# Two transformer blocks on one core: three stick-breaking half chunks between the delta net's last two transposings, and two small pieces of work moved to later steps

## The chip, the cores and the metric

The kernel runs on one core of one Trainium2 chip. The metric is the device time of one execution in microseconds, shown as the median of three runs. A core has five engines that run side by side and meet only through semaphores: TensorE (PE in the profile, its weight loads PEld), VectorE (DVE), ScalarE (ACT), GpSimd (POOL) and SyncE (SP), which here issues nearly all DMA transfers, in order.

## The reference

The input is 256 tokens of 1024 values, with 16 meta tokens put in front; everything is float32. The first block is a hybrid mixer and a mixture of experts, the second has attention, a pooling mixer and two MLPs. What matters here is the mixer:

```python
proj = x @ w_in
q = l2_normalize(split_heads(q, DN_HEADS)) * (DN_HEAD_DIM ** -0.5)
o_dn = gated_delta_rule_chunked(front(q), front(k), front(v), front(beta), front(g))[:, :, pad:]
o_dn = merge_heads(rms_norm(o_dn, dn_norm_g)) * jax.nn.silu(dn_z.astype(jnp.float32))
o_sb = merge_heads(stick_breaking_attention(q, k, v))
gate = jax.nn.sigmoid(gates.reshape(b, l, N_BRANCH, d) + b_gate)
merged = (gate[:, :, 0] * (o_dn @ w_branch_dn) + gate[:, :, 1] * (o_sb @ w_branch_sb))
return merged @ w_out
```

The delta net (4 heads of 128) and the stick-breaking attention (8 heads of 64) are two branches over the same tokens. Each goes through a projection of its own, `w_branch_dn` and `w_branch_sb`. After a layer norm, 32 experts follow, of which each token takes two.

## The kernel before

Weights stream from memory in chunks of 1 MB (`wraw`), each of two halves. A half is split before use: ACT rounds it to a high part (L324) and DVE takes the remainder (L326); both lie in one of two `wsplit` buffers, and a product is three matmuls (high by high, low by high, high by low: L374, L375, L376). So a half is 24 matmuls, the split of a half waits until the half two places before it has been used, and a chunk's place in the ring is free once its second half is split. SP loads five chunks ahead.

The mixer has three generators, advanced in one loop (L1052 on), a step of each per turn `it`. `F` is the projections that are left (the fill: halves of 24 matmuls that keep PE busy). `M` is the delta net: for two chunks of 128 tokens (and the meta tokens) it builds a triangular matrix, inverts it by seven levels of doubling (`invert`: GpSimd masks the blocks, PE multiplies and transposes, ACT and DVE evacuate), and then walks the two chunks. `sticks` are the four pairs of stick-breaking heads: PE makes the scores, ACT takes exp, exp and log, DVE adds (L923) and scans (L927), GpSimd subtracts (L928), ACT takes exp (L929), PE transposes (L936) and multiplies (L944 to L948).

The root of q's norms, `rq`, is ten small instructions on DVE (`rsqrt`, L437 to L446, and a product, L812). It is written in the step that makes q's norms, although its first reader is the end of a chunk (L894). `router_weights()` folds the first layer norm into the expert router's weights: four matmuls (L994) and five DVE instructions (L995 to L998). It is called in turn 2, and its result is read when the experts begin.

After the loop, each chunk's result `oraw` is multiplied by the gate `zr` (L1069, DVE), transposed (L1072, PE) and split (`odh`, `odl`). `BS_AT` says which of the four half chunks of `w_branch_sb` stand behind the first of these two transposings and which behind the second: `for i in range(BS_AT[c], BS_AT[c + 1])`. With (0, 1, 1) one stands between them and three follow the second. Each of them ends in two evacuations on DVE (`sb_evac`, L957). Eight half chunks of gates follow, then the delta net's branch, the output projection, the layer norm and the experts.

The experts' weights (`wexp`, 99 loads of 1 MB) go into 22 places, which come free one after another while the mixer ends. When all 22 are full, the next load waits for PE to have used the first.

The order on each engine is not that of the code: a scheduler places instructions by their dependencies and its costs, and `tc.issue_after` holds one back until another has been issued. Each engine runs its own list strictly in order.

Of the kernel before, what the change touches and what calls it, by code (L numbers as in the profile page):

```python
# [14 lines left out]
OP = mybir.AluOpType  # L15
# [31 lines left out]
DEPTH = 3  # L47
PARTS = (1, 2, 4, 6, 8)
G_ELSE = (1, 4, 6)
BS_AT = (0, 1, 1)  # L50
COUNT_AT = 0
DN_STEPS = (3, 5, 10, 11, 11)
DN_FILL = (7, 9)
ALPHA = float(np.float32(2.0 ** 0.25))
# [228 lines left out]
def tile_hybrid_block(ctx: ExitStack, tc: tile.TileContext, A, out, dump=None, stop=99):  # L283
    nc = tc.nc
    V, S, G, PE = nc.vector, nc.scalar, nc.gpsimd, nc.tensor
# [36 lines left out]
    def split_into(hi, lo, src, sub=None, after=(None, None)):  # L322
        with tc.issue_after(after[0].ins) if after[0] else nullcontext():
            S.copy(hi, src)  # L324
        with tc.issue_after(after[1].ins) if after[1] else nullcontext():
            (sub or V).tensor_tensor(lo, src, hi.bitcast(F32), op=OP.subtract)  # L326
# [40 lines left out]
    def ws_half(stream, m0, nk, xh, xl, width, fn, newbank):  # L367

        wh, wl = stream.half()
        for q in range(8 // nk):  # L370
            p = newbank()
            for k in range(nk):
                o = (q * nk + k) * 128
                PE.matmul(p[:, :width], wh[:, o:o + 128], xh[:, k, :], start=k == 0, stop=False)  # L374
                PE.matmul(p[:, :width], wl[:, o:o + 128], xh[:, k, :], start=False, stop=False)  # L375
                PE.matmul(p[:, :width], wh[:, o:o + 128], xl[:, k, :], start=False, stop=k == nk - 1)  # L376
            fn(m0 + q, p)
# [53 lines left out]
    def rsqrt(x, shape):  # L431
        P, n = shape
        y = small.tile([128, 12], F32, tag="rs_y", name="rs_y")[:P, :n]
        z = small.tile([128, 12], F32, tag="rs_z", name="rs_z")[:P, :n]
        t = small.tile([128, 12], F32, tag="rs_t", name="rs_t")[:P, :n]
        ti = small.tile([128, 12], I32, tag="rs_i", name="rs_i")[:P, :n]
        V.tensor_scalar(ti, x.bitcast(I32), 1, None, op0=OP.arith_shift_right)  # L437
        V.tensor_scalar(y.bitcast(I32), ti, -1.0, float(0x5F1FFFF9), op0=OP.mult, op1=OP.add)
        V.tensor_tensor(t, y, y, op=OP.mult)
        V.tensor_tensor(t, t, x, op=OP.mult)  # L440
        V.scalar_tensor_tensor(z, t, -RS_A, y, op0=OP.add, op1=OP.mult)
        V.tensor_tensor(t, z, z, op=OP.mult)
        V.tensor_tensor(t, t, x, op=OP.mult)
        V.tensor_scalar(y, t, RS_Q[0], RS_Q[1], op0=OP.mult, op1=OP.add)
        V.tensor_tensor(y, y, t, op=OP.mult)
        V.scalar_tensor_tensor(y, y, RS_Q[2], z, op0=OP.add, op1=OP.mult)  # L446
        return y
# [153 lines left out]
    mark = {}  # L601
# [87 lines left out]
    def delta():  # L689
# [72 lines left out]
        for c in range(2):  # L762
# [7 lines left out]
            for h in range(4):  # L770
                V.scalar_tensor_tensor(di[c][:, HS[h]], pd[:, HS[h]], pc[c][:, 32 + h:33 + h], C("nincl"),
                                       op0=OP.subtract, op1=OP.add)
# [8 lines left out]
        for c in range(2):  # L781
# [7 lines left out]
            for h in range(4):  # L789
                V.scalar_tensor_tensor(At[:, HS[h]], pk[:, HS[h]], pc[c][:, h:h + 1], ds_[:, HS[h]],  # L790
                                       op0=OP.mult, op1=OP.mult)
# [4 lines left out]
        rq = mix.tile([128, 8], F32, name="rq")  # L796
# [11 lines left out]
                PE.matmul(pn[:, c * 4 + h:c * 4 + h + 1], sq[:, META + c * 128:META + c * 128 + 128],  # L808
                          C("ones")[:, 0:1], start=True, stop=True)
        V.tensor_scalar(rq, pn[:, :8], 1e-6, None, op0=OP.add)  # L810
        rq = rsqrt(rq, (128, 8))
        V.tensor_scalar(rq, rq, float(128.0 ** -0.5), None, op0=OP.mult)  # L812

        G.memset(mv_, 0.0)
        G.tensor_copy(mv_.rearrange("p (h c) -> p h c", c=32)[:, :, :16], cvv[:, :, :16])
# [9 lines left out]
        S.copy(mrow, p[:, :256].rearrange("p (a d) -> p a d", d=128))  # L825
        yield
        XTs = [None] * 3
        live = [0, 1, 2]
        while live:
            for i in list(live):  # L830
                r = next(gens[i])
                if r is not None:
                    XTs[i] = r
                    live.remove(i)
            yield
# [16 lines left out]
        for c in range(2):  # L852
# [5 lines left out]
            for h in range(4):  # L858
                V.scalar_tensor_tensor(nR[:, HS[h]], pks[:, HS[h]], pc[c][:, 64 + h:65 + h], vr[c][:, h, :],
                                       op0=OP.mult, op1=OP.subtract)  # L860
# [14 lines left out]
            if c == 0:  # L875
# [4 lines left out]
                for h in range(4):  # L880
                    V.scalar_tensor_tensor(Sn[:, HS[h]], Sst[:, HS[h]], edl[:, c, h:h + 1], pS[:, HS[h]],
                                           op0=OP.mult, op1=OP.add)
# [103 lines left out]
    def router_weights():  # L986

        t = mix.tile([128, 2, 288], F32, tag="zt", name="wr2")
        k36 = lambda a: a.rearrange("p (k n) -> p k n", n=36)
        for q, n in enumerate(("ln1g", "ln1b")):  # L990
            o = _VCOLS[n][0]
            V.tensor_tensor(k36(t[:, q, :]), k36(wrt), colv[:, o:o + 8, None].to_broadcast([128, 8, 36]), op=OP.mult)
            p = bank()
            PE.matmul(p[:, :288], C("ones"), t[:, q, :], start=True, stop=True)  # L994
            V.tensor_reduce(rcb[:, q, :], p[:, :288].rearrange("p (k n) -> p n k", n=36), axis=AX.X, op=OP.add)  # L995
        V.tensor_scalar(rcb[:, 0, :], rcb[:, 0, :], 1.0 / D, None, op0=OP.mult)
        V.tensor_tensor(rcb[:, 1, :], rcb[:, 1, :], rb, op=OP.add)
        V.tensor_tensor(k36(wrt), k36(t[:, 0, :]), rcb[:, None, 0, :].to_broadcast([128, 8, 36]), op=OP.subtract)  # L998
# [14 lines left out]
    def prefetch(n):  # L1013

        while exn[0] < 99 and len(exq) < n and sn[0] - n_slots < (exq[0][0] if exq else sn[0]):
            if ring3[0][0] is None and sn[0] >= 4 + N_RING2:
                break
            i = exn[0]
            exn[0] += 1
            num, t = sn[0], slot()  # L1020
            with tc.issue_after(last_load[0].ins) if last_load[0] else nullcontext():
                if 0 <= i - 12 * SPARE_AT < 3:
                    last_load[0] = spare_load[0](t, i - 12 * SPARE_AT)
                else:
                    g, k = divmod(i if i < 12 * SPARE_AT else i - 3, 12)
                    last_load[0] = nc.sync.dma_start(t, A["wexp"][g, k].rearrange("p e n -> p (e n)"))
            exq.append((num, t))
# [3 lines left out]

    sticks = []
    M = delta()
    F = fill()
    ws_front(wpre, DN_ORDER[:FRONT], hh, hl, T, dn_evac, bank)
    for n, m in enumerate(DN_ORDER):
# [4 lines left out]
        if n in DN_FILL:  # L1041
            next(F)
        for _ in range(DN_STEPS.count(n)):
            next(M)
# [5 lines left out]
    m_on = f_on = True  # L1050
    it = 0
    while m_on or f_on or sticks:  # L1052
        if it == 2:
            router_weights()
        if it >= 8:
            with tc.issue_after(mark["DVE"].ins):
                next(residual_steps, None)
        it += 1
        if m_on:
            m_on = next(M, "end") != "end"  # L1060
        if f_on:
            f_on = next(F, "end") != "end"
        sticks[:] = [s for i, s in enumerate(sticks) if i >= N_STICKS or next(s, "end") != "end"]
        if it > 12 and not sticks and not exq:
            prefetch(4)

    oraw = ofin[0]
    for c in range(2):
# [4 lines left out]
        split_into(odh[:, :, c * 128:(c + 1) * 128], odl[:, :, c * 128:(c + 1) * 128], v3(p))  # L1073
        for i in range(BS_AT[c], BS_AT[c + 1]):
            ws_half(wpre, 2 * i, 4, osh, osl, SEQ, sb_evac, bank)
# [8 lines left out]

    for i in range(BS_AT[2], 4):
        ws_half(wpre, 2 * i, 4, osh, osl, SEQ, sb_evac, bank)
# [74 lines left out]
    def tt(o, a, b, op):  # L1161
# [9 lines left out]
                           op0=OP.is_ge, op1=OP.mult)  # L1171
# [63 lines left out]
    def count_blocks():  # L1235
        cnt = rt([32], "cnt", tag="xact")
        nb = rt([32], "nb", tag="xoff")
        pc_ = bank4()
        PE.matmul(pc_[:, 0:32], C("ones"), msk_[:, 0:32], start=True, stop=False)
        PE.matmul(pc_[:, 0:32], C("ones"), msk_[:, 32:64], start=False, stop=True)  # L1240
        V.tensor_copy(cnt, pc_[:, 0:32])
        V.tensor_scalar(nb, cnt, float(CAP), None, op0=OP.is_gt)
        for m_ in range(2, SEQ // CAP):
            V.scalar_tensor_tensor(nb, cnt, float(CAP * m_), nb, op0=OP.is_gt, op1=OP.add)
        V.tensor_tensor_scan(ci, nb, nb, 0.0, op0=OP.add, op1=OP.bypass)
        tt(cx, ci, nb, OP.subtract)
        V.tensor_scalar(n_ext, ci[0:1, 31:32], -1.0, 0.0, op0=OP.add, op1=OP.max)
        V.memset(ctr, 0.0)
# [219 lines left out]
    for g in range(NG):  # L1468
# [10 lines left out]
        for k in range(8):  # L1479
# [5 lines left out]
            for e in range(4):  # L1485
                behind[0] = PE.matmul(pg[32 * e:32 * e + 32, :], xt[:, k, 32 * e:32 * e + 32], w[:, e, :],  # L1486
                                      start=k == 0, stop=k == 7).ins
            if g == 0 and k == COUNT_AT:
                count_blocks()
# [71 lines left out]
        if g == NG - 3:  # L1561

            for o, op in ((lg, OP.mult), (lb, OP.add)):
                for q in range(2):
# [4 lines left out]
                    for c in range(2):  # L1569
                        hs_ = slice(q * 512, (q + 1) * 512)  # L1570
                        V.scalar_tensor_tensor(res[:, c, hs_], p, ALPHA, (h0 if op == OP.mult else res)[:, c, hs_],
                                               op0=OP.mult, op1=op)
# [40 lines left out]
    for k in range(8):  # L1613
# [3 lines left out]
                                     op0=OP.mult, op1=OP.subtract)  # L1617
# [367 lines left out]
```

## Time and profile before

| what | value |
|---|---|
| median of three runs (1010.31 to 1011.78) | 1011.24 us |
| the profiled execution | 1012.06 us |
| its span, first to last instruction | 1010.3 us |
| PE busy | 944.3 us, 93% |
| DVE busy | 603.7 us, 60% |
| ACT busy | 483.4 us, 48% |
| mean granted clock of TensorE | 0.979 of full |
| moved by DMA | 227.32 MB |

The span is 1.76 us shorter than the profiled execution's time; the rest lies before the first and after the last instruction. A share of busy time is a mean over stages that have different limits, so the stages are read one by one: where PE waits, for what, and where the DMA engines are full.

### The profile page before, as it was taken

The page shows a single profiled execution, that of the slowest core. Times are in us where ns is not written, and L with a number is a line of the kernel's source. Part 1 is how long each engine was busy: PE and PEld are TensorE (multiplying, and loading weights), DVE is VectorE, ACT ScalarE, POOL GpSimd, SP SyncE. Part 2 cuts the span into 40 slices and gives each one's busy share as a digit, 9 for nine tenths or more (in the row PEclk, how much of TensorE's full clock was granted, in tenths as well). Part 3 has the DMA queues.
Part 4 walks back from the last instruction along what each step waited for, and adds up shares of the span by engine and source line. Part 5 has one row for each costly group of instructions (what it writes and reads, how often), then busy time and mean ns, then how long its engine had stood idle before and what let it go on. Part 6 is the DMA issues. An engine that isn't in the chain of part 4 may idle for free.

```text
span 1010.3 us, 14882 instructions
## 1 busy us (share of the span) xinstructions
PE 944.3 (93%) x5905; PEld 757.5 (75%) x5905; DVE 603.7 (60%) x1163; ACT 483.4 (48%) x846; POOL 68.3 (7%) x60
## 2 busy tenths in 40 slices
PE   6997999989999999987789999999999999999996
PEld 5996997989884534442368889888888788888885
DVE  7887564664863312231186777756666686666664
ACT  4855576434432111101155565755555576555552
POOL 0004232000300000000020001000000020000002
PEclk9999999999999999999989999999999999999999
DMA  9440223649689999999865434555555525555521
GB/s 363 165 165 1 90 84 121 249 187 355 249 315 406 416 425 423 426 423 426 352 236 179 167 126 176 180 174 201 180 195 182 193 84 209 184 191 182 193 84 42
DMA packets 34231, 227.32 MB, mean 225 GB/s; under 512 B 3936, under 2 KB 4704, under 8 KB 7664
## 3 DMA queue, kind: packets, MB, share of 16 engines
q1 hardware_dynamic: 34160, 226.36, 58.8%
q8 instruction: 47, 0.77, 0.3%
q14 instruction: 24, 0.20, 0.1%
HBM read 225.29 MB, written 1.05 MB: 224 GB/s over the span
## 4 chain that ended last, share of the span: by engine, by line
PE 72%; DMA 16%; DVE 6%; ACT 3%; POOL 2%; issue 1%; SPq 0%; POOLq 0%; ACTq 0%; DVEq 0%
DMA wexp<-in_wexp_dram 14%; PE bank L385 11%; PE bank L386 6%; PE acc L1831 6%; PE acc L1832 6%; PE acc L1833 6%; PE bank L375 5%; PE bank L376 5%; PE bank L374 5%; PE bank L413 3%; PE bank L414 3%; PE bank L412 3%; DMA wraw<-in_wpost_dram 2%; PE bank L1486 1%; DVE wsplit L326 1%; PE bank L674 1%
## 5 line engine op out<-in xcount | busy, mean ns | idle before, releaser
L326 DVE TENSOR_TENSOR wsplit<-wraw,wsplit 128x1024 fp32r<-128x1024 f32 x222 | 277.7, 1251 | 143.5 <-ACT wsplit L324 139.5
L324 ACT CAST wsplit<-wraw 128x1024 fp32r<-128x1024 f32 x222 | 233.0, 1051 | 144.8 <-PE acc L1833 79.7
L385 PE MATMUL bank<-xx,wsplit 128*128 128x512 f32 x512 | 179.0, 393 | 2.2 <-DVE xx L1598 2.2
L386 PE MATMUL bank<-xx,wsplit 128*128 128x256 f32 x512 | 142.8, 280 | 0.7 <-DVE wsplit L326 0.7
L385 PEld LDWEIGHTS bank<-xx,wsplit 128*128 128x128 f32 x512 | 96.1, 188 | 24.4 <-DVE xx L1598 3.5
L1831 PE MATMUL acc<-wsplit,mhh 128*128 128x512 f32 x256 | 100.5, 393 | 0.0
L1832 PE MATMUL acc<-wsplit,mhh 128*128 128x512 f32 x256 | 99.8, 390 | 0.0
L1833 PE MATMUL acc<-wsplit,mhl 128*128 128x512 f32 x256 | 99.7, 390 | 0.0
L386 PEld LDWEIGHTS bank<-xx,wsplit 128*128 128x128 f32 x512 | 96.2, 188 | 1.6 <-DVE wsplit L326 1.0
L375 PE MATMUL bank<-hh,wsplit 128*128 128x256 f32 (+1 forms) x304 | 88.4, 291 | 2.7 <-DVE wsplit L326 2.7
L374 PE MATMUL bank<-hh,wsplit 128*128 128x256 f32 (+1 forms) x304 | 89.6, 295 | 0.0
L376 PE MATMUL bank<-hl,wsplit 128*128 128x256 f32 (+1 forms) x304 | 87.7, 289 | 0.0
L1486 PE MATMUL bank<-wexp,xt 128*32 128x512 f32 x512 | 62.8, 599 | 5.3 <-DMA wexp<-in_wexp_dram 4.3
L375 PEld LDWEIGHTS bank<-hh,wsplit 128*128 128x128 f32 x304 | 58.6, 193 | 3.6 <-DVE wsplit L326 3.2
L374 PEld LDWEIGHTS bank<-hh,wsplit 128*128 128x128 f32 x304 | 58.7, 193 | 0.4 <-issue 0.2
L376 PEld LDWEIGHTS bank<-hl,wsplit 128*128 128x128 f32 x304 | 58.7, 193 | 0.0
L1833 PEld LDWEIGHTS acc<-wsplit,mhl 128*128 128x128 f32 x256 | 48.1, 188 | 10.1
L1832 PEld LDWEIGHTS acc<-wsplit,mhh 128*128 128x128 f32 x256 | 48.1, 188 | 9.9 <-DVE wsplit L326 0.3
L1831 PEld LDWEIGHTS acc<-wsplit,mhh 128*128 128x128 f32 x256 | 48.1, 188 | 9.7
L1816 ACT COPY relu<-bank 128x256 f32<-128x256 f32 x64 | 23.8, 373 | 62.8 <-PE bank L386 62.7
L1512 ACT ACTIVATE hid<-bank 128x256 f32<-128x256 f32 x8 | 3.1, 383 | 89.1 <-PE bank L1486 89.1
L1460 PE MATMUL bank<-wexp,hT 128*32 128x512 f32 x256 | 32.6, 624 | 9.8 <-DMA wexp<-in_wexp_dram 4.2
(542 smaller groups left out, 1648.8 us busy)
## 6 DMA issues: line engine op xcount, KB each, us to landing
wexp<-in_wexp_dram SPq DMA_DIRECT2D x99, 1024.0 KB, 19.6
wraw<-in_wpost_dram SPq DMA_DIRECT2D x81, 1024.0 KB, 4.7
wraw<-in_wpre_dram SPq DMA_DIRECT2D x30, 1024.0 KB, 4.9
h<-in_x_dram SPq DMA_DIRECT2D x2, 512.0 KB, 4.4
eb<-in_rowv_dram SPq DMA_DIRECT2D x2, 512.0 KB, 10.7
out_dram<-of SPq DMA_DIRECT2D x4, 256.0 KB, 2.1
cpre<-in_cst_dram SPq DMA_DIRECT2D x1, 915.5 KB, 10.3
pmat<-in_poolm_dram SPq DMA_DIRECT2D x1, 544.0 KB, 3.2
```

The source lines that it names most:

```text
L324: S.copy(hi, src)
L326: (sub or V).tensor_tensor(lo, src, hi.bitcast(F32), op=OP.subtract)
L374: PE.matmul(p[:, :width], wh[:, o:o + 128], xh[:, k, :], start=k == 0, stop=False)
L375: PE.matmul(p[:, :width], wl[:, o:o + 128], xh[:, k, :], start=False, stop=False)
L376: PE.matmul(p[:, :width], wh[:, o:o + 128], xl[:, k, :], start=False, stop=k == nk - 1)
L385: PE.matmul(p, wh[:, o], xx[:, k].rearrange("p q t -> p (q t)"), start=k == 0, stop=False)
L386: PE.matmul(p[:, :SEQ], wl[:, o], xx[:, k, 0], start=False, stop=k == 7)
L1460: behind[0] = PE.matmul(py[32 * e:32 * e + 32, sl], hT[:, i, 32 * e:32 * e + 32], w[:, e, sl], start=i == 0, stop=i == 1).ins
L1486: behind[0] = PE.matmul(pg[32 * e:32 * e + 32, :], xt[:, k, 32 * e:32 * e + 32], w[:, e, :], start=k == 0, stop=k == 7).ins
L1831: PE.matmul(ac[c][n], hh_, wh, start=g == 0 and k == 0, stop=False)
L1832: PE.matmul(ac[c][n], hh_, wl, start=False, stop=False)
L1833: PE.matmul(ac[c][n], hl_, wh, start=False, stop=g == 7 and k == 3)
```

## The change

Four constants and two moves. `BS_AT` becomes (0, 3, 3): three half chunks of `w_branch_sb` stand between the two transposings, one behind the second. `ROUTER_AT = 7`: `router_weights()` is called in turn 7. `RQ_AT = 4`: the root of q's norms is made in the fourth turn of the inversions, behind the last subtraction that `invert` issued.

```diff
-BS_AT = (0, 1, 1)
+BS_AT = (0, 3, 3)
 COUNT_AT = 0
+ROUTER_AT = 7
+RQ_AT = 4
...
         V.tensor_scalar(rq, pn[:, :8], 1e-6, None, op0=OP.add)
-        rq = rsqrt(rq, (128, 8))
-        V.tensor_scalar(rq, rq, float(128.0 ** -0.5), None, op0=OP.mult)
...
-        live = [0, 1, 2]
+        live, n_live = [0, 1, 2], 0
         while live:
+            n_live += 1
+            if n_live == RQ_AT:
+                with tc.issue_after(mark["DVE"].ins):
+                    rq = rsqrt(rq, (128, 8))
+                    V.tensor_scalar(rq, rq, float(128.0 ** -0.5), None, op0=OP.mult)
...
-        if it == 2:
+        if it == ROUTER_AT:
             router_weights()
```

Line numbers in the change are two higher up to q's norms and five higher from the inversions' loop on (L326 becomes L328, L923 becomes L928, L1069 becomes L1074).

On DVE, where the first stick's scans stand (`sbwork`; `rs_t`, `rs_y` are the root, `rcb` and `wrt` the router, `wsplit` a remainder of the fill), before:

```order
L443 TENSOR_TENSOR rs_t<-rs_t,rq 128x8
L995 TENSOR_REDUCE rcb<-bank 128x36
L444 TENSOR_SCALAR rs_y<-rs_t 128x8
L996 TENSOR_SCALAR rcb<-rcb 128x36
L997 TENSOR_TENSOR rcb<-rcb,cpre 128x36
L445 TENSOR_TENSOR rs_y<-rs_y,rs_t 128x8
L998 TENSOR_TENSOR wrt<-wr_1111,rcb 128x288
L446 SCALAR_TENSOR_TENSOR rs_y<-rs_y,rs_z 128x8
L326 TENSOR_TENSOR wsplit<-wraw,wsplit 128x1024
L812 TENSOR_SCALAR rs_y<-rs_y 128x8
L326 TENSOR_TENSOR wsplit<-wraw,wsplit 128x1024
```

And there in the change, from the last product of `di` on:

```order
L805 TENSOR_TENSOR di_916<-bank,di_916 128x512
L928 SCALAR_TENSOR_TENSOR sbwork<-sbwork 128x832
L328 TENSOR_TENSOR wsplit<-wraw,wsplit 128x1024
L932 SCALAR_TENSOR_TENSOR sbwork<-sbwork 128x144
L932 SCALAR_TENSOR_TENSOR sbwork<-sbwork 128x272
L932 SCALAR_TENSOR_TENSOR sbwork<-sbwork 128x144
L932 SCALAR_TENSOR_TENSOR sbwork<-sbwork 128x272
L328 TENSOR_TENSOR wsplit<-wraw,wsplit 128x1024
```

The first remainder stood behind the scans, the root and the router's five instructions; now it stands ahead of the scans, and the root and the router are gone from here.

On DVE at the mixer's end (`rs_y` is the root of the second chunk's norms, `oraw` its rows, `gg_246` the stick-breaking branch), before:

```order
L444 TENSOR_SCALAR rs_y<-rs_t 128x4
L445 TENSOR_TENSOR rs_y<-rs_y,rs_t 128x4
L446 SCALAR_TENSOR_TENSOR rs_y<-rs_y,rs_z 128x4
L898 SCALAR_TENSOR_TENSOR rs_y<-rs_y 128x4
L899 TENSOR_TENSOR oraw<-oraw,rs_y 128x512
L1069 TENSOR_TENSOR oraw<-oraw,zr 128x512
L326 TENSOR_TENSOR odl<-bank,odh 128x4x128
```

And there in the change:

```order
L962 SCALAR_TENSOR_TENSOR gg_246<-gg_246,bank 128x256
L446 TENSOR_SCALAR rs_y<-rs_t 128x4
L447 TENSOR_TENSOR rs_y<-rs_y,rs_t 128x4
L962 SCALAR_TENSOR_TENSOR gg_246<-gg_246,bank 128x256
L448 SCALAR_TENSOR_TENSOR rs_y<-rs_y,rs_z 128x4
L903 SCALAR_TENSOR_TENSOR rs_y<-rs_y 128x4
L904 TENSOR_TENSOR oraw<-oraw,rs_y 128x512
L328 TENSOR_TENSOR wsplit<-wraw,wsplit 128x1024
L962 SCALAR_TENSOR_TENSOR gg_246<-gg_246,bank 128x256
L1074 TENSOR_TENSOR oraw<-oraw,zr 128x512
```

Three evacuations of the half chunks and one remainder now stand ahead of L1074, the product that the second transposing needs.

On SP, the loads of the mixer's weights (`wraw`) and of the experts' (`wexp`), before:

```order
L319 DMA wraw<-in_wpre_dram 128x2048 x5
L1026 DMA wexp<-in_wexp_dram 128x2048 x2
L319 DMA wraw<-in_wpre_dram 128x2048
L1026 DMA wexp<-in_wexp_dram 128x2048
L319 DMA wraw<-in_wpre_dram 128x2048
L1026 DMA wexp<-in_wexp_dram 128x2048
```

And in the change, with the row that ends the stretch:

```order
L321 DMA wraw<-in_wpre_dram 128x2048 x6
L1031 DMA wexp<-in_wexp_dram 128x2048 x2
L321 DMA wraw<-in_wpre_dram 128x2048
L1031 DMA wexp<-in_wexp_dram 128x2048
L321 DMA wraw<-in_wpre_dram 128x2048 x2
L1031 DMA wexp<-in_wexp_dram 128x2048
L321 DMA wraw<-in_wpre_dram 128x2048
L1031 DMA wexp<-in_wexp_dram 128x2048
L321 DMA wraw<-in_wpre_dram 128x2048
L1031 DMA wexp<-in_wexp_dram 128x2048 x13
```

A sixth load of `wraw` now stands ahead of the two of `wexp`, and the last group of `wexp` has 13 loads where it had 12.

## Rows read from the trace of the kernel before

**Rows 1.** The page: the chain that ended last, shares by engine.

```profile
PE 72%; DMA 16%; DVE 6%; ACT 3%; POOL 2%; issue 1%; SPq 0%; POOLq 0%; ACTq 0%; DVEq 0%
```

**Rows 2.** Busy time per stretch: engines (instructions), granted clock, DMA share, GB/s.

```profile
100.00:105.00 5.00, 4.05 (x21) 4.05 (x21) 2.25 (x5) 0.00 (x0) 0.00 (x0) 0.66 0.56 210
130.00:135.00 5.00, 5.00 (x45) 4.77 (x45) 0.31 (x1) 4.86 (x7) 2.58 (x2) 1.00 0.02 5
...
215.00:220.00 5.00, 2.61 (x13) 2.64 (x14) 2.70 (x7) 0.59 (x1) 0.00 (x0) 0.68 1.01 428
295.00:300.00 5.00, 4.17 (x34) 3.06 (x33) 2.40 (x13) 0.46 (x1) 0.00 (x0) 0.97 0.33 126
...
350.00:400.00 50.00, 47.04 (x286) 17.71 (x279) 10.20 (x24) 8.95 (x19) 0.00 (x0) 1.00 1.01 424
```

**Rows 3.** Timeline of PE, first sticks: start, duration, line [idle before <-releaser].

```profile
85.33 1.13 PE L994 MATMUL bank<-wr,cst 128*128 128x288 f32 x4
...
89.61 0.63 PE L652 MATMUL bank<-cst,XT 128*128 128x128 f32 x4 [2.51 <-DVE XT L656]
...
96.53 0.37 PE L374 MATMUL bank<-hh,wsplit 128*128 128x272 f32 x1
98.56 0.33 PE L936 MATMUL bank<-cst,sbwork 128*128 128x128 f32 x1 [1.66 <-ACT sbwork L929]
100.95 0.59 PE L375 MATMUL bank<-hh,wsplit 128*128 128x272 f32 x1 [2.06 <-DVE wsplit L326]
...
105.24 0.29 PE L376 MATMUL bank<-hl,wsplit 128*128 128x272 f32 x1
...
107.67 0.49 PE L674 MATMUL bank<-inv_u,XTm 128*128 128x128 f32 x2
```

**Rows 4.** Timeline of DVE, the same stretch.

```profile
89.98 0.86 DVE L437 TENSOR_SCALAR rs_i<-rq 128x8 int32<-128x8 int32 x1
90.76 1.01 DVE L923 SCALAR_TENSOR_TENSOR sbwork<-sbwork 128x832 f32<-128x832 f32 x1
...
92.14 0.15 DVE L439 TENSOR_TENSOR rs_t<-rs_y 128x8 f32<-128x8 f32 x1
...
94.81 1.78 DVE L444 TENSOR_SCALAR rs_y<-rs_t 128x8 f32<-128x8 f32 x1
...
113.70 1.03 DVE L923 SCALAR_TENSOR_TENSOR sbwork<-sbwork 128x832 f32<-128x832 f32 x1 [2.78 <-ACT sbwork L921]
```

**Rows 5.** Timeline of POOL, the same stretch.

```profile
94.61 1.96 POOL L928 TENSOR_TENSOR sbwork<-sbwork 128x832 f32<-128x832 f32 x1 [3.79 <-DVE rs_t L443]
```

**Rows 6.** Timeline of ACT, the same stretch.

```profile
97.61 0.90 ACT L929 ACTIVATE sbwork<-sbwork 128x832 f32<-128x832 f32 x1
```

**Rows 7.** Timeline of PE at the mixer's end.

```profile
212.24 0.28 PE L376 MATMUL bank<-osl,wsplit 128*128 128x256 f32 x1
217.39 1.09 PE L1072 MATMUL bank<-cst,oraw 128*128 128x128 f32 x4 [4.87 <-DVE oraw L1069]
...
222.00 0.28 PE L374 MATMUL bank<-osh,wsplit 128*128 128x256 f32 x1
...
227.69 0.28 PE L374 MATMUL bank<-hh,wsplit 128*128 128x256 f32 x1
```

**Rows 8.** Timeline of DVE at the mixer's end.

```profile
211.62 0.41 DVE L957 SCALAR_TENSOR_TENSOR gg<-gg,bank 128x256 f32<-128x256 f32 x1
...
213.64 1.23 DVE L326 TENSOR_TENSOR wsplit<-wraw,wsplit 128x1024 fp32r<-128x1024 f32 x1
...
216.56 0.69 DVE L1069 TENSOR_TENSOR oraw<-oraw,zr 128x512 f32<-128x512 f32 x1
```

**Rows 9.** Timeline of SP, the DMA issues: start, time until the last, line.

```profile
211.54 0.86 SPq L1026 DMA_DIRECT2D wexp<-in_wexp_dram  x2
...
253.97 38.23 SPq L1026 DMA_DIRECT2D wexp<-in_wexp_dram  x12
...
300.09 22.17 SPq L1026 DMA_DIRECT2D wexp<-in_wexp_dram  x14
```

## The prediction

> **What bounds the kernel now.** I read the page's chain of waits first. It gives PE 72% of the span and DMA 16% [rows 1]. So a microsecond in which PE stands idle is a microsecond of the whole, except in the experts' stage, where the DMA engines are full: a share of 1.01 at 424 GB/s over 50 us [rows 2]. The next views are therefore the timelines of PE around the places that the change touches, read for the brackets that name a wait, and then the engines named there.
>
> Two places carry losses. At the first stick, PE waits 1.66 us for the exp of ACT (L929) with one transposing (L936), then 2.06 us for a remainder of DVE (L326) [rows 3]. The clock granted in this stretch falls to 0.66, a mean of 2.4 and 1.2 GHz [rows 2], and the half that should take 3 us runs until 105.37 (the last matmul starts at 105.24). The remainder is late because DVE runs its list in order: scans, root and router stand ahead of it. At the mixer's end PE waits 4.87 us for `oraw` (L1069), with the granted clock at 0.68 for the 5 us after [rows 2, 7].
>
> How a change here reaches the end of the program is shown by SP. The experts' 22 places are full at about 295 + 0.33 x 5 = 296.7 us [rows 2], and the next load is issued at 300.09, when PE has used the first [rows 9]. DMA therefore idles 3.4 us and is then the bound. The experts' end hangs on that first use, thus on PE, as long as the places are full before it.
>
> **The first stick.** In the change the remainder stands between L923 and the scans. L923 ends at 91.77 as now: before it only L437 is gone, which ended when a GpSimd instruction did. The remainder takes 1.23 us [rows 8], so it is done at 93.0. PE needs it at 96.53 [rows 3]: the 2.06 us wait goes. What is late next is the exp: the scans take at most the 2.84 us that lie between 91.77 and POOL's start at 94.61 [rows 4, 5], now from 93.0 to 95.9; POOL's subtraction takes 1.96 [rows 5], to 97.8; the exp takes 0.90 [rows 6], to 98.7. PE, by its list, asks for the exp only behind the whole half. A half of 256 columns takes (227.69 - 222.00) / 2 = 2.85 us [rows 7], one of 272 columns 2.85 x 272/256 = 3.02. So the half ends at 96.53 + 3.02 = 99.55, 0.8 us after the exp; that is the cover. From the end of this half (105.37) to L674 (107.67) PE now needs 2.30 us [rows 3], and one L936 (0.11) joins. L674 thus starts at 99.55 + 2.41 = 101.96 instead of 107.67: **5.7 us** won, low clock included. If POOL is held up and the exp comes a microsecond later, 0.2 of it is lost.
>
> Here a rule bears. The root's L444 took 1.78 us from 94.81, L439 of the same width 0.15; L444 ended at 96.59, just when POOL's L928 did, 94.61 + 1.96 = 96.57 [rows 4, 5]. The Trainium skill (SBUF — State Buffer, "Who interferes with whom") says that VectorE and GpSimd take a port pair as an exclusive lock, and that a VectorE instruction with two SBUF inputs waits for a GpSimd instruction that reads SBUF, or the other way round, whoever came first. By that rule the second remainder may hold POOL for its 1.23 us; the exp then ends at 99.9, and PE loses 0.4 us of the 5.7. By the rows alone it loses nothing.
>
> **The root.** Its ten instructions move to where DVE now idles 2.78 us before the second stick's L923 at 113.70 [rows 4]. Eight stand ahead of L923: 8 x 0.15 = 1.2 us if each is as long as L439, hidden by that idle time. If L437 (0.86) and L444 (1.78) kept their lengths there, the eight would take 3.5 us and the stick would be 0.8 us late. I take the short ones, since the long ones ended with POOL. One more stands between L923 and the scans and delays the stick, which PE waits for a little later: I take **0.2 us lost**; the bounds are 0 and 0.8.
>
> **The router.** Its four matmuls take 1.13 us at 85.33 and lie ahead of a wait of 2.51 us that another chain ends [rows 3]; there they are free, and taking them away wins nothing. At the new place, a stick later, PE has no free time: 5.00 of 5.00 us busy at 130 to 135 [rows 2]. **1.1 us lost.** The five DVE instructions go into a stretch in which DVE is busy for 0.31 of 5 us [rows 2]: nothing. The wait at 89.61 becomes 3.6 us; whether PE's clock then stays low longer no row shows. I bound that by 0 and 1.4, what the low clock cost the half after the 2.06 us wait (4.42 us for 23 matmuls instead of 3.02), and take 0.
>
> **The mixer's end.** Now: the one half chunk ends at 212.24 + 0.12 = 212.36 and the gates begin at 227.69, 15.33 us later [rows 7]. In that are three halves (8.55), the wait to 217.39 (5.03), the transposing (0.55 at full clock, half of 1.09), and about 1.2 us of low clock. In the change halves two and three run on from 212.36 to 218.06, inside the old wait; the low clock goes with it. What is late next is L1069, for DVE has to do more ahead of it, in order. The second evacuation of half two cannot start before that half ends (212.36 + 2.85 + 0.3 = 215.5). From there: 0.41 for it, two small ones at 0.15, `oraw` times the root as long as L1069 (0.69), the remainder 1.23, one evacuation 0.41, L1069 itself 0.69 [rows 4, 8]. That is 3.7 us, to 219.2. PE waits 1.1 us for it instead of 5.03, then takes 0.55 for the transposing and 2.85 for the last half: the gates begin at 222.6. **5.1 us won.** The bounds are 6.2 (no wait) and 3.1 (DVE 2 us later).
>
> **The sum.** 5.7 - 0.2 - 1.1 + 5.1 = 9.5 us, before the experts. It passes through them whole if their places are still full before PE's first use. That asks for the last group of loads to come at least 9.5 + 2.5 - 3.4 = 8.6 us earlier, as it has one load more, of 1.05 MB / 424 GB/s = 2.5 us. It should: the twelve issues are spread over 38.23 us [rows 9], 3.2 each, so they wait for places that PE, DVE and POOL set free, not for DMA, and these come earlier as PE does. The profiled execution took 1012.06 us, of which 1.76 lie around the span; less 9.5 it is 1002.6. It lies 0.8 above the median of the runs shown, so I predict 1011.24 - 9.5 = **1001.7 us**.
>
> **Rivals**, counted from the median.
>
> - DVE is later than my chain at the mixer's end (a cast of ACT that waits for the buffer of half two, say). With 2 us more, PE waits 3.1 us and the clock falls again for about 1 us: 6.5 won, 1004.7. For it: seven DVE instructions in a row, each dependent or behind a wait. Against: my chain is serial throughout.
> - At the first stick the exp is the bound, not the remainder: scans, POOL and ACT together 2 us later than reckoned. PE then waits 1.2 us at 99.55 and the clock falls (1.4): 6.9 won, 1004.3. For it: POOL and DVE held each other up here before [rows 4, 5]. Against: 0.8 us of cover.
> - The DMA keeps most of it: the last group ends where it ends now, plus its one load, 299.2. Only 0.9 us is won, 1010.3. Against: the spread of the twelve issues.
> - Slower: the loads move back on SP, in order. A sixth load of the mixer stands ahead of the two at 211.54, and it waits for a remainder of DVE, which now stands behind more work. If this costs the last group two load times beyond the one load more, it ends at 296.7 + 3 x 2.5 = 304.2, DMA has no idle time left, and the experts start 4.1 us late: 1015.3. It decides from 300.1 on. Against: places that come free earlier.
>
> **How the numbers follow.** The forecast 62%, with a range of its own from 999.3 (11.9 won: no wait at the mixer's end, and nothing lost to root and router) to 1003.5; DVE late 14%; exp late 10%; DMA keeps it 7%; slower 4%; 3% that gain and loss cancel for a reason that I do not see. The range from 999.3 to 1006.0 holds the first three, with a little beyond for two of them at once. A run can tell 0.2% (2 us) from no change. Faster by more has 62 + 14 + 10 and half of the DMA case, 0.90; the same has 0.06; slower 0.04.
>
> **What would show it.** In the new profile PE should have no wait for a remainder at the first stick, L674 (now L676) should start near 102, and the granted clock between 95 and 100 should be full. L1077 should wait about 1 us near 214.8 (219.2 less 4.4), with no low clock behind it. The gates should begin near 218.2, and the load that follows the 22 near 290.6, with idle DMA ahead of it. I am wrong if one of these waits stays above 2 us, or if DMA is already full when PE reaches the experts.

## The result, and the profile after

The changed kernel took 999.82 us (median of four runs, 999.12 to 1000.22) against 1011.34 for the kernel before on the same chip: a ratio of 0.9886, interval 0.9874 to 0.9898. Timed again later beside other kernels it took 1001.01 against 1010.60, 0.9907 (0.9892 to 0.9923). The forecast was 1001.7. The two profiled executions (1012.06 and 999.6 us) lie 12.5 us apart. The change has three constants, not four: `BS_AT`, `ROUTER_AT` and `RQ_AT`.

The page's chain of the changed kernel, where [rows 1] had 72% and 16%:

```profile
PE 73%; DMA 14%; DVE 6%; ACT 3%; POOL 2%; issue 1%; SPq 0%; ACTq 0%; POOLq 0%; DVEq 0%
```

PE around the first sticks, which answers to [rows 3]:

```profile
88.62 1.12 PE L654 MATMUL bank<-cst,XT 128*128 128x128 f32 x4 [3.05 <-DVE XT L658]
93.59 0.38 PE L668 MATMUL bank<-Xm,inv_b 128*128 128x128 f32 x2
...
95.52 0.37 PE L376 MATMUL bank<-hh,wsplit 128*128 128x272 f32 x1
95.73 0.29 PE L377 MATMUL bank<-hh,wsplit 128*128 128x272 f32 x1
...
98.49 0.29 PE L378 MATMUL bank<-hl,wsplit 128*128 128x272 f32 x1
98.62 0.49 PE L941 MATMUL bank<-cst,sbwork 128*128 128x128 f32 x3
...
101.04 0.49 PE L676 MATMUL bank<-inv_u,XTm 128*128 128x128 f32 x2
```

Both waits of [rows 3], 1.66 and 2.06 us, are gone: the half runs from 95.52 to 98.62 without a bracket, and the stick's transposings follow at once.

DVE in the same stretch, which answers to [rows 4]:

```profile
89.09 1.71 DVE L928 SCALAR_TENSOR_TENSOR sbwork<-sbwork 128x832 f32<-128x832 f32 x1
90.73 1.21 DVE L328 TENSOR_TENSOR wsplit<-wraw,wsplit 128x1024 fp32r<-128x1024 f32 x1
91.86 2.02 DVE L932 TENSOR_TENSOR_SCAN sbwork<-sbwork 128x144 f32<-128x144 f32 x4
95.32 2.20 DVE L328 TENSOR_TENSOR wsplit<-wraw,wsplit 128x1024 fp32r<-128x1024 f32 x1 [1.44 <-ACT wsplit L326]
...
104.04 0.15 DVE L439 TENSOR_SCALAR rs_i<-rq 128x8 int32<-128x8 int32 x1
...
106.89 1.03 DVE L928 SCALAR_TENSOR_TENSOR sbwork<-sbwork 128x832 f32<-128x832 f32 x1 [1.28 <-ACT sbwork L926]
...
111.44 1.62 DVE L834 TENSOR_SCALAR rs_y<-rs_y 128x8 f32<-128x8 f32 x1
```

POOL there, which answers to [rows 5]:

```profile
94.47 1.97 POOL L933 TENSOR_TENSOR sbwork<-sbwork 128x832 f32<-128x832 f32 x1
```

ACT, which answers to [rows 6]:

```profile
96.60 0.90 ACT L934 ACTIVATE sbwork<-sbwork 128x832 f32<-128x832 f32 x1
```

The remainder that PE needs behind 95.52 is done at 91.94. The exp ends at 97.50, 1.1 us before PE asks for it. The eight instructions of the root that stand ahead of the second stick's L928 take 0.15 to 0.17 us each, in DVE's idle time.

PE at the mixer's end, which answers to [rows 7]:

```profile
212.28 0.28 PE L378 MATMUL bank<-osl,wsplit 128*128 128x256 f32 x1
213.43 0.63 PE L1077 MATMUL bank<-cst,oraw 128*128 128x128 f32 x4 [0.88 <-DVE oraw L1074]
```

DVE there, which answers to [rows 8]:

```profile
209.81 0.41 DVE L962 SCALAR_TENSOR_TENSOR gg<-gg,bank 128x256 f32<-128x256 f32 x1
...
210.52 0.69 DVE L904 TENSOR_TENSOR oraw<-oraw,rs_y 128x512 f32<-128x512 f32 x1
211.13 1.22 DVE L328 TENSOR_TENSOR wsplit<-wraw,wsplit 128x1024 fp32r<-128x1024 f32 x1
212.27 0.41 DVE L962 SCALAR_TENSOR_TENSOR gg<-gg,bank 128x256 f32<-128x256 f32 x1
212.60 0.68 DVE L1074 TENSOR_TENSOR oraw<-oraw,zr 128x512 f32<-128x512 f32 x1
```

PE waits 0.88 us instead of 4.87, behind the serial chain of DVE that the prediction listed: from the start of half two's second evacuation (209.81) to the end of L1074 (213.28) it takes 3.5 us, reckoned 3.7.

The table of stretches (columns as in [rows 2]) around these places, and where the experts' loads begin:

```profile
95.00:100.00 5.00, 5.00 (x44) 4.87 (x43) 2.29 (x2) 4.61 (x7) 4.92 (x3) 1.00 0.22 90
...
215.00:220.00 5.00, 5.00 (x45) 5.00 (x44) 2.56 (x4) 1.20 (x2) 0.00 (x0) 1.00 1.00 416
...
286.00:288.00 2.00, 1.90 (x16) 0.87 (x16) 1.02 (x5) 0.46 (x1) 0.00 (x0) 1.00 0.07 25
288.00:290.00 2.00, 2.00 (x20) 1.45 (x20) 1.25 (x7) 0.46 (x1) 0.00 (x0) 1.00 0.37 74
...
350.00:400.00 50.00, 47.63 (x286) 18.83 (x279) 9.31 (x21) 6.85 (x15) 0.00 (x0) 1.00 1.01 423
```

And SP's issues, which answer to [rows 9]:

```profile
212.80 0.86 SPq L1031 DMA_DIRECT2D wexp<-in_wexp_dram  x2
...
243.00 38.34 SPq L1031 DMA_DIRECT2D wexp<-in_wexp_dram  x13
...
288.01 22.16 SPq L1031 DMA_DIRECT2D wexp<-in_wexp_dram  x14
```

Behind the mixer's end the granted clock is 1.00, where it was 0.68. The last group of the experts' loads begins 10.97 us earlier (243.00 for 253.97) with its one load more. DMA is idle from 286 to 288 (a share of 0.07), so the places were full before PE's first use; the load after them is issued at 288.01, 12.1 us earlier than at 300.09. The whole gain passes.

**Where the 12.5 us lie.** I cut every profiled execution at the same four events: PE's one wait for a remainder near 42 us (L377), the wait of some 1.57 us for `inv_u` near 157 (L676), the third wait for a remainder behind the experts' norm near 259 (L415), and the first L1266 near 286. The lines are those of the changed kernel; in the kernel before the same instructions are L375, L674, L413 and L1261. The change lies between the first and the third. Differences of start times, in us, the last column being the rest of the span:

```
kernel               to L377  to L676  to L415  to L1266    rest    span
before                42.60   119.94   107.62    27.58   712.56  1010.3
changed               41.71   115.16   102.36    26.42   712.15   997.8
changed, again        41.30   115.19   102.35    26.40   712.06   997.3
half chunks alone     42.19   121.06   102.37    27.60   711.98  1005.2
root and router       42.44   115.25   107.89    27.60   712.62  1005.8
root alone            42.16   114.88   107.90    27.57   712.39  1004.9
router alone          42.73   115.70   108.17    26.39   711.51  1004.5
router in turn 2      42.39   114.90   102.32    26.42   711.47   997.5
router in turn 12     42.27   114.14   102.34    26.38   713.27   998.4
four half chunks      42.07   115.23   101.22    27.64   712.74   998.9
two half chunks       40.97   115.16   104.88    27.61   712.38  1001.0
four, router in 12    42.22   114.15   101.25    26.44   711.34   995.4
router in turn 6      42.18   114.19   102.33    27.63   712.67   999.0
```

The second and third columns hold 4.78 + 5.26 = 10.04 us of the change. The other 2.5 us (0.89 + 1.16 + 0.41) lie where no instruction was moved. The runs below show that they go with no part of the change.

### The profile page after: what moved, and what is told of

Read it like the earlier page. It is cut to its first block, busy times and chain, and to the rows that moved or that the text cites. A ratio compares the mean times of both kernels' runs of the same rounds, so it can differ in the third digit from the quotient of the medians.

```text
span 997.8 us, 14883 instructions
## 1 busy us (share of the span) xinstructions
PE 939.5 (94%) x5905; PEld 752.7 (75%) x5905; DVE 602.1 (60%) x1163; ACT 483.7 (48%) x846; POOL 68.5 (7%) x60
## 3 DMA queue, kind: packets, MB, share of 16 engines
HBM read 225.29 MB, written 1.05 MB: 227 GB/s over the span
## 4 chain that ended last, share of the span: by engine, by line
PE 73%; DMA 14%; DVE 6%; ACT 3%; POOL 2%; issue 1%; SPq 0%; ACTq 0%; POOLq 0%; DVEq 0%
DMA wexp<-in_wexp_dram 12%; PE bank L387 11%; PE bank L388 6%; PE acc L1836 6%; PE acc L1837 6%; PE acc L1838 6%; PE bank L377 5%; PE bank L378 4%; PE bank L376 4%; PE bank L415 3%; PE bank L416 3%; PE bank L414 3%; PE bank L1491 2%; DMA wraw<-in_wpost_dram 2%; PE bank L1266 2%; DVE wsplit L328 1%
## 5 line engine op out<-in xcount | busy, mean ns | idle before, releaser
L328 DVE TENSOR_TENSOR wsplit<-wraw,wsplit 128x1024 fp32r<-128x1024 f32 x222 | 277.7, 1251 | 143.7 <-ACT wsplit L326 139.8
L326 ACT CAST wsplit<-wraw 128x1024 fp32r<-128x1024 f32 x222 | 232.9, 1050 | 143.5 <-PE acc L1838 79.7
L377 PE MATMUL bank<-hh,wsplit 128*128 128x256 f32 (+1 forms) x304 | 87.4, 287 | 0.6 <-DVE wsplit L328 0.6
L377 PEld LDWEIGHTS bank<-hh,wsplit 128*128 128x128 f32 x304 | 57.8, 190 | 1.3 <-DVE wsplit L328 1.0
```

## The experiments

### Each part alone

Only the half chunks, root and router as before:

```diff
-BS_AT = (0, 1, 1)
+BS_AT = (0, 3, 3)
```

> Only the half chunks are moved (three between the transposings, one behind); the router's weights stay in turn 2 and the root of q's norms in its old step. My theory: the gain at the mixer's end is a thing of its own, 5.3 us there (wait for oraw 0.9 us instead of 4.9, no low clock behind it), and all of it reaches the end: about 1006.0 against 1011.3. The first stick keeps its waits of 1.66 and 2.06 us. Rival: the mixer's end gains only because the stages ahead of it run earlier (the experts' loads, DVE's queue): then under 3 us, over 1008.3. The profiled changed kernel was ahead by 0.9 us more at the start (granted clock) and by 1.2 us more at the matmuls that wait for the experts' weights (granted clock); if these come from the change of the order they belong to one of its parts: 1004.8 if the second goes with the half chunks, 1006.0 if it is a difference between single executions.

Measured: 1006.63 us, ratio 0.9958 (0.9943 to 0.9973), 4.6 us. The stretch to L415 is 102.37, the changed kernel's own value: 5.25 us won there, with a wait of 0.88 us. My theory holds, the rival falls. The median shows less gain than that. In the profiled execution the old waits of the first stick (1.66 and 2.01 us) cost 1.1 us more than in the kernel before, since the clock stayed low longer behind the second of them:

```profile
100.00:105.00 5.00, 4.48 (x20) 4.48 (x21) 1.82 (x5) 0.00 (x0) 0.00 (x0) 0.50 0.57 210
105.00:110.00 5.00, 5.00 (x38) 4.32 (x38) 2.66 (x4) 2.59 (x6) 0.00 (x0) 0.86 0.00 0
```

In the kernel before the clock of the first of these stretches was 0.66 [rows 2] and that of the second was full.

Root and router, half chunks as before:

```diff
-        if it == 2:
+        if it == ROUTER_AT:      # 7; and the root in turn 4
```

> Only the root and the router's weights are moved; the half chunks stand as before, one between the transposings. My theory: 5.6 us won at the first stick, 0.1 at the second, 1.06 lost for the router's four matmuls, thus 4.6: about 1006.7. The mixer's end keeps its wait of about 4.9 us with the low clock behind it. If the start's 0.9 us comes with this part, 1005.8. Rival: the two parts feed each other (the experts' loads need both to come early), then under 3 us here and the two parts alone sum to less than the whole of 11.5.

Measured: 1006.79 us, 0.9949 (0.9935 to 0.9963), 4.5 us. To L676 115.25, within 0.1 of the changed kernel; the mixer's end keeps its wait of 4.87. Each counted in its own stretch, the parts add up on PE: 4.69 + 5.25 = 9.94 against 10.04 for both. Behind the wait that each part keeps, its execution was slower than the kernel before: by 1.12 us up to L676 with half chunks alone, by 0.27 up to L415 here.

The root alone (router in turn 2, half chunks as before):

```diff
+            if n_live == RQ_AT:      # the root in turn 4, router still in turn 2
```

> Only the root is moved; the router's weights stay in turn 2. On DVE the first remainder of the fill then stands behind the scans and two reduces of the router, still ahead of the router's last two. My theory (GpSimd and DVE hold each other up): the scans are done near 94.0, GpSimd's subtraction starts ahead of the remainder and holds it for about 1.97 us, so that it ends near 97.2 instead of the 95.5 at which PE asks: a wait of 1.0 to 1.7 us is left, with some low clock behind it. Won 3.5 to 4.5 us at the first stick, nothing lost to the router: about 1007.3. Rival, without such a hold: the remainder ends at 95.5, nothing is waited for, 5.6 us are won and the router's matmuls stay free ahead of a wait: 1005.7, better than root and router moved together. A second rival, that the router's instructions alone keep the remainder: no more than 1 us won, 1010.5.

Measured: 1005.99 us, 0.9940 (0.9925 to 0.9956). PE waits 0.41 us for the remainder, and 5.06 us are won to L676. So the second rival falls, the first holds nearly, and my theory named the mechanism but overrated its size. DVE in this run:

```profile
93.80 1.87 DVE L1001 TENSOR_SCALAR rcb<-rcb 128x36 f32<-128x36 f32 x1
95.59 1.21 DVE L328 TENSOR_TENSOR wsplit<-wraw,wsplit 128x1024 fp32r<-128x1024 f32 x1
```

POOL beside it:

```profile
93.67 1.95 POOL L933 TENSOR_TENSOR sbwork<-sbwork 128x832 f32<-128x832 f32 x1 [3.34 <-DVE sbwork L932]
95.59 1.52 POOL L648 TENSOR_TENSOR inv_b<-Am,cpre 128x128 f32<-128x128 f32 x1
```

It is the router's small L1001 that POOL's subtraction holds, until 95.6; the remainder stands behind it, and then holds POOL in its turn (L648 takes 1.52, in the changed kernel 0.46).

The router alone (root in its old step):

```diff
-        if it == 2:
+        if it == ROUTER_AT:      # 7; the root not moved
```

> Only the router's weights are moved to turn 7; the root stays in its old step. On DVE the first remainder then stands ahead of the scans, and the root's products stand between the scans. My theory: the remainder is in time, the scans end about 1.1 us later than in the changed kernel (L439 at 0.86, some products at 0.15), the exp ends at 98.6 instead of 97.5, when PE asks for it at 98.6: 5.6 won, 1.06 lost, 1006.8, the same as with the root moved as well. Rival: the products of the root are held by GpSimd's subtraction, and with them the second remainder behind them, which PE then waits for 1 to 2 us: 1008.5. If so the root's move is worth some 1.7 us, otherwise nothing.

Measured: 1006.15 us, 0.9954 (0.9938 to 0.9970). L676 behind the first stick starts 59.36 us after L377, in the changed kernel 59.33: the first stick's gain is whole. Of the root, three instructions are held by POOL, whose subtraction ends at 97.52 and whose next two (L648) end at 100.02. DVE in this run:

```profile
95.66 1.90 DVE L446 TENSOR_SCALAR rs_y<-rs_t 128x8 f32<-128x8 f32 x1
97.59 1.21 DVE L447 TENSOR_TENSOR rs_y<-rs_y,rs_t 128x8 f32<-128x8 f32 x1
98.83 1.21 DVE L448 SCALAR_TENSOR_TENSOR rs_y<-rs_y,rs_z 128x8 f32<-128x8 f32 x1
```

The second remainder comes late behind them (100.43 to 101.65), but not too late, so the rival falls. The price is paid a stick later: the second stick's L921 (L923 in the changed kernel) stands behind this remainder on DVE and starts 60.57 us after L377 instead of 59.95, and PE waits 1.08 us for `inv_u` instead of 0.56:

```profile
116.05 2.13 PE L676 MATMUL bank<-inv_u,XT 128*128 128x128 f32 x16 [1.08 <-ACT inv_u L670]
```

The root's move is worth 0.5 us once the router is gone. Either move alone frees the first remainder; the two together win 4.78 to L676, less than the root alone (5.06), since the router's matmuls cost 1.06 in turn 7.

### The whole again, and the router's place

> The changed kernel itself, timed beside the others. The parts alone gave 4.6 (half chunks) and 4.5 us (root and router); the whole gave 11.5 in another set of runs. Theory one: the parts are independent and the excess of some 2 us lay in which executions had low granted clock at the start and at the matmuls that wait for the experts' weights; then it comes out at 1001 to 1002 here. Theory two: the parts help each other; then again 999.8, and the profile shows the start's and the waiting matmuls' clock full once more.

Measured: 1001.01 us (999.11 to 1001.95), 0.9907 (0.9892 to 0.9923), 9.6 us. Theory one holds for the times; where the clock was low in the slower executions is not shown, as only one was profiled. The profiled execution is again one with full clock in both places, which theory two had asked for, but it was the fastest of the four: the others, with a mean granted clock of 0.984 and 0.982 for its 0.987, took 1000.23, 1001.79 and 1001.95.

```diff
-ROUTER_AT = 7
+ROUTER_AT = 2
```

> The changed kernel with the router's weights back in turn 2. Root alone had shown that the remainder then comes 0.4 us late, while the router's four matmuls (1.06 us) lie ahead of a wait. My theory: PE is 0.3 us ahead of the changed kernel from the second stick on, and 0.3 us faster at the end, hardly to be told from it. Rival: the move of the router is needed for the gain at the first stick: over 4 us slower than the changed kernel.

Measured: 1001.80 us, 0.9915 (0.9902 to 0.9929), not to be told from the changed kernel in time. To L676 it is 0.29 us ahead of it (114.90 for 115.19): the late remainder (a wait of 0.42 us) costs it 0.78 us up to the second stick, the router's matmuls cost the changed kernel 1.06. The move of the router is not needed for the gain.

```diff
-ROUTER_AT = 7
+ROUTER_AT = 12
```

> The changed kernel with the router's weights in turn 12: on PE their four matmuls then stand directly ahead of the L676 that waits 1.57 us for inv_u. My theory: the 1.06 us that they cost in turn 7 lie in that wait, which becomes 0.5 us: 1.06 us faster than the changed kernel. Rival: their five DVE instructions land where DVE is on the path to that same wait, and it moves with them: no gain, or a loss of up to 1 us.

Measured: 999.47 us, 0.9889 (0.9873 to 0.9904). The two intervals overlap, so the time alone does not tell it from the changed kernel; the stretch on PE does. The wait is 0.58 us instead of 1.57, and L676 starts 1.05 us earlier:

```profile
154.69 1.14 PE L999 MATMUL bank<-wr,cst 128*128 128x288 f32 x4
156.41 0.82 PE L676 MATMUL bank<-inv_u,XT 128*128 128x128 f32 x5 [0.58 <-ACT inv_u L670]
```

```diff
-ROUTER_AT = 7
+ROUTER_AT = 6
```

> The changed kernel with the router's weights in turn 6: on PE its four matmuls stand ahead of the L676 that waits 0.56 us for inv_u. My theory: of their 1.06 us 0.56 lie in that wait and 0.5 remain; PE is 0.5 us ahead of the changed kernel from the second stick on. Rival: its DVE instructions fall beside the second stick's scans and GpSimd's subtraction, which hold them for up to 2 us, and DVE delays that same product: 0 to 1 us behind the changed kernel.

Measured: 1000.36 us, 0.9884 (0.9867 to 0.9902). To L676 0.97 us are won, twice what I expected. PE in this run:

```profile
114.03 1.14 PE L999 MATMUL bank<-wr,cst 128*128 128x288 f32 x4
115.00 0.38 PE L676 MATMUL bank<-inv_u,XTm 128*128 128x128 f32 x2
115.22 1.95 PE L676 MATMUL bank<-inv_u,XT 128*128 128x128 f32 x16
```

The same two groups in the changed kernel:

```profile
113.53 0.38 PE L676 MATMUL bank<-inv_u,XTm 128*128 128x128 f32 x2
114.48 2.13 PE L676 MATMUL bank<-inv_u,XT 128*128 128x128 f32 x16 [0.56 <-ACT inv_u L670]
```

The bracket of 0.56 is not all the room. The two small matmuls ahead of it take 0.95 us to the next start instead of 0.22, and the sixteen behind it 2.13 instead of 1.95, since they wait once more inside the group. 0.73 + 0.18 is 0.91 us that the router fills. The gain is read from this stretch; the median does not tell the two kernels apart.

### The number of half chunks

```diff
-BS_AT = (0, 3, 3)
+BS_AT = (0, 4, 4)
```

> The changed kernel with all four half chunks between the two transposings and none behind. The product oraw is done at 213.3 in the changed kernel and PE is through with three halves at 212.55; the fourth lasts 2.85 us. My theory: the wait of 0.88 us goes and nothing comes in its place: 0.9 us faster than the changed kernel, and the second transposing 2 us later. Rival: the loads of the mixer's and the experts' weights fall back by one place on SP (the mixer's last load then stands behind one more of the experts'), the last group comes later, and the experts' loads keep 0.5 to 2.5 us of it: the same or slower.

Measured: 999.08 us, 0.9883 (0.9868 to 0.9898), an interval that still overlaps that of the changed kernel beside it. L1077 follows the fourth half without a wait:

```profile
215.53 0.28 PE L378 MATMUL bank<-osl,wsplit 128*128 128x256 f32 x1
215.65 0.60 PE L1077 MATMUL bank<-cst,oraw 128*128 128x128 f32 x4
```

To L415 PE takes 101.22 us, 1.13 less than the changed kernel; the loads keep none of it up to there, and the last group again has 13. The 0.25 above the wait are a loss of changing over that I had not reckoned and do not take apart.

```diff
-BS_AT = (0, 3, 3)
+BS_AT = (0, 2, 2)
```

> The changed kernel with two half chunks between the transposings and two behind. My theory: DVE's list up to the product of oraw and the gate is the same but for one evacuation, so it starts near 212.3 and PE, done with two halves near 209.7, waits about 3.3 us instead of 0.9, perhaps with low clock behind it: 2.5 to 3.5 us slower than the changed kernel, 1003.5 to 1004.5. So each half chunk moved ahead is worth its own length until the wait is full. Rival: with fewer evacuations ahead of it the product comes early by as much as the half is long, the wait stays near 1 us, and the number of half chunks does not matter beyond two: the same as the changed kernel.

Measured: 1003.73 us, 0.9935 (0.9920 to 0.9950), 2.7 us above the changed kernel's second median. PE:

```profile
212.35 0.63 PE L1077 MATMUL bank<-cst,oraw 128*128 128x128 f32 x4 [3.39 <-DVE oraw L1074]
```

The product's time hangs on DVE's chain, not on how many halves PE has done, and the stretch to L415 grows by 2.53 us, a half chunk less the 0.33 of the evacuation that L1074 no longer stands behind. The rival falls.

The two better choices together:

```diff
-BS_AT = (0, 3, 3)
+BS_AT = (0, 4, 4)
-ROUTER_AT = 7
+ROUTER_AT = 12
```

> All four half chunks between the transposings and the router's weights in turn 12, the two changes that won 1.13 and 1.03 us on PE apart. My theory: they lie in different stretches and add: from the first wait for a remainder (near 42) to the third product behind the experts' norm (L415, 259.2 in the changed kernel) PE takes 215.4 us against 217.5, and the time is 2.1 us below the changed kernel's, near 998.5 to 998.9. Rival: the experts' 22 places are no longer full before PE's first use, since the last load comes only behind more of the mixer's; then under 1 us of it arrives.

Measured: 997.51 us (997.13 to 998.96), 0.9871 (0.9854 to 0.9888), the lowest median of all, and 1 us below the expectation. Its interval lies clear of the changed kernel's second one (0.9892 to 0.9923), not of its first (0.9874 to 0.9898), so the 2.1 us rest on the stretches. From L377 to L415 PE takes 114.15 + 101.25 = 215.40 us, as expected. The load after the 22 is issued at 286.42 with a DMA share of 0.14 from 284 to 286, so the places were still full in time.

## Why the prediction was right

**First stick: 5.7 us, measured 5.74.** From L377's wait to L674 it was 107.67 - 42.60 = 65.07 us, to L676 it is 101.04 - 41.71 = 59.33. The remainder was the step that failed before, and the exp, named as next, is 1.1 us early instead of 0.8. That the gain is met to 0.04 us is in part luck: the prediction took the low clock from the same execution of the kernel before, and with half chunks alone, which keeps nearly the same waits, L676 comes 66.28 us after L377, 1.2 later. In one thing the case that I weighed did not come: by the Trainium skill (SBUF — State Buffer, "Who interferes with whom") the second remainder would have held POOL, if it had come first. Here POOL came first, at 94.47, and the remainder, begun at 95.32, took 2.20 us instead of 1.21, ending 1.1 us behind POOL. So the rule holds in its other direction, and PE lost nothing by it. The remainder, which reads `wraw` and `wsplit`, is the case of two inputs that the prediction named; L444, which it set beside the rule, reads one.

**Root: 0.2 lost, measured nothing.** Between L676 and the second stick's wait 13.54 us became 13.44, but with half chunks alone, where the root is not moved, it is 13.45 too. The eight instructions were short as taken. The tenth, L834, was held for 1.62 us (111.44, by the second stick's subtraction on POOL), and no loss shows on PE. What the step missed is that the root would have cost 0.5 us in its old place, with the router gone, as the run without its move shows.

**Router: 1.1 lost, measured 1.06.** Here the prediction saw only that the old place was free; the runs show that places with as much room lay ahead of two later waits.

**Mixer's end: 5.1 won, measured 5.26** to L415; the wait is 0.88 us instead of the 1.1 reckoned, and the low clock behind it is gone.

**Passed whole.** The load after the 22 comes 12.1 us earlier, with idle DMA before it. It comes at 288.01 where the prediction had 290.6; 0.89 + 1.16 us of the difference lie in the first and fourth columns, outside the change.

The terms sum to 10.04 us where the prediction had 9.5. The first comparison gave 11.5, the second 9.6. That the first came close to the best case of the prediction, 999.3, is luck: what that case stood for, no wait at the mixer's end, did not happen. The surplus is in no term. In the table, the first, fourth and fifth columns take values that go with no part of the change. To L377, where all thirteen run the same work, they spread from 40.97 to 42.73, and the changed kernel itself has 41.71 and 41.30. In the fourth column there are two values, 26.4 and 27.6. They go with the 28 matmuls that fill PE's wait behind the router's product, which take 3.37 us in the six runs with 26.4 and 4.79 to 5.00 in the seven with 27.6. In the changed kernel:

```profile
280.78 3.37 PE L509 MATMUL bank<-cst 128*128 128x128 f32 x28
```

and in the kernel before

```profile
291.64 5.00 PE L507 MATMUL bank<-cst 128*128 128x128 f32 x28
```

In the five microseconds from their start the granted clock is 1.00 (2.4 GHz) in the changed kernel and 0.66, a mean of 2.4 and 1.2 GHz, in the kernel before. The kernel with the router alone has 26.39 and the one with the root alone 27.57; with four half chunks it is 27.64, and with the router in turn 12 as well 26.44. So neither root, router nor half chunks decide it. What does was not settled.

The gain itself also differs by execution, since what the low clock costs behind the old waits does. Of all profiles that keep such a wait, that of the kernel before has the shortest stretch: 119.94 us to L676 against 121.06 with half chunks alone, and 107.62 to L415 against 107.89, 107.90 and 108.17 in the three kernels with the old half chunks. So the 10.04 us may lie at the low end, and part of the surplus here; with one profile of the kernel before this is not shown.

The rivals with DVE or the exp late fall by the waits of 0.88 and 0 us; the two with DMA by its idle time at 286.

## What to carry to other kernels

When PE is the bound, follow the late operand back along the engine that makes it, and ask which small instructions stand ahead of it in that engine's order; ten instructions of 8 columns and five of the router, together with the scans, had kept PE waiting 2 us, with the low clock behind, and taking away either group freed it (all but 0.4 us). Work that can stand anywhere goes directly ahead of a wait that another chain ends, and the room there can be more than the wait, by the broken overlap around it: 1.0 us of router went into a wait of 0.56. Compare kernels by stretches between common events before adding up whole times: here the whole varied by 2.8 us within one kernel, the stretches that the change touches by 0.03 between its two profiles. Where a long wait with low clock behind it lies in the stretch, that does not hold: the same waits gave values 1.1 us apart.

## What the runs showed of the hardware

- **Executions of one kernel differ, in part by where the clock is low.** The changed kernel, with its mean granted clock at 0.987, 0.984 and 0.982, took 999.11, 1000.23 and 1001.79 us. In its two profiles the clock from 15 to 20 and from 20 to 25 was 0.68 and 0.98 in one, 1.00 and 1.00 in the other; the same matmuls ended 0.41 us apart. But the mean clock does not settle the time: with the root alone two executions at 0.989 took 1004.58 and 1006.73 us.
- **Not each wait is followed by low clock.** Behind the wait of 3.39 us, with two half chunks, the clock from 212 to 221 was 1.00; behind 4.87 us it was 0.68 in the kernel before [rows 2], and 0.76 from 210 to 215 with root and router alone. Nor is it the shorter wait that has full clock behind it: after the wait of 3.05 us at 88.62 in the changed kernel the clock from 88.6 to 93.6 was 0.67. Behind the same wait of 4.87 us, the way from the transposing to the gates took 10.30 us in the kernel before, 10.55 with root and router alone and 10.88 with the router alone.
- **An engine's small instruction can take eleven times its length.** L446, 128x8, took 1.90 us beside POOL's subtraction and 0.17 alone; the hold also goes the other way, as L648's 1.52 for 0.46 shows.
